# Preparing weight sums ahead of time: nine sets instead of seven, issued by GpSimd

## The chip, the cores and the metric

One core of a Trainium2 chip runs the whole program. The core has a matrix engine (PE in the profile), a vector engine (DVE), a scalar engine (ACT), GpSimd (POOL), and SyncE (SP), whose work here is to issue transfers. Every engine executes its own list of instructions strictly in order; what one engine must wait for from another, it waits for at a semaphore. Transfers run on 16 DMA engines, whoever issues them. The metric is the device time of one execution in microseconds (us), as the median of several executions; lower is better.

## The reference: what is computed

One transformer layer over 256 tokens of width 2048, in float32, with three kinds of attention that share one projection, gates, and a gated feed-forward part:

```
z   = split_cols(h @ w_in)                                   # queries, keys, values, gates
mix = g_fox * (fox(z) @ w_br_fox) + g_nsa * (nsa(z) @ w_br_nsa) + g_dsa * (dsa(z) @ w_br_dsa)
h   = layer_norm(ALPHA * h + mix @ w_out)
a, b = split(h @ w_ffn_in, 2)                                # each 5632 columns
h   = layer_norm(ALPHA * h + (silu(a) * b) @ w_ffn_out)
h   = h + (p @ w_ple_in) * sigmoid(h @ w_ple_gate)
```

What this case is about is the product `h @ w_ffn_in` and what the attention stage does ahead of time for it.

## The kernel before, in words

**Precision and the triple product.** Every float32 operand is split into a high half and a low half (`halves`, L154: ACT copies the high half, DVE subtracts it to get the low half). A product is then three matmuls: high x high, low x high, high x low. All weights pass through this split, so DVE and ACT have work for each weight tile that PE uses.

**Groups of weights.** `gemm` (L207) walks through the 2048 rows of a weight matrix in groups of two blocks of 128 rows (1024 columns of a tile, or 768 where the matrix is 384 columns wide). For each group it loads the raw weights (`weight_group`, L158, on SP's queue), splits them and issues the matmuls. At the end of each group it calls `tick()` (L182), which lets side work advance by one step. Side work is written as Python generators: `yield n` means "come back n groups later". So one group of weights is the unit in which all side work is spread. The attention stage has 121 groups: 57 of the chunks c1 to c7, 48 of the chunks f0 to f5 (one for each fox head) and 16 of `gates(0)`. The lists `side` (attention heads and the like, three at a time) and `beside` (the preparation) hold the generators.

The program text gives the order of priority only. The order in which each engine's list is finally written is fixed at compile time by a planner that may move an instruction ahead of others on its engine when it expects its operands to be there. So side work can run well before the group at which it is written.

**Pairs with seven products.** `pair_gemm` (L279) multiplies the same input by two weight matrices at once (for the feed-forward part, 512 columns of `a` and 512 columns of `b`, a "chunk"). It takes the 2048 rows as eight pairs `p` of 128-row blocks. For each pair there are 2 x 2 blocks of tokens and rows, and 2 weight matrices: eight block products, 24 matmuls, in the plain way (`plain`, L340). For the pairs named in `seven` it uses a scheme with seven block products (L391 to L397), 21 matmuls. In exchange, sums and differences of weights have to be formed and split: four DVE additions (L380 to L382) and more `halves`.

The feed-forward part has chunks 0 to 10. Chunk 0 is made by `first_chunk`; chunks 1 to 10 by `next_chunk` (L1205), which chooses the pairs that go the seven-product way: `SEVEN` = (2, 4, 6) for chunk 1, `SEVEN_MOST` = (2, 3, 4, 5, 6) for a chunk that has a prepared set, and `SEVEN_MORE` = (2, 4, 5, 6) otherwise.

**Prepared sets.** For some chunks the sums of pair 2 are formed early, in the attention stage, by `prepare` (L891), and kept in DRAM. One set (c, p) takes three tiles of 128 x 1024 floats, `preb`, `prea` and `pret`: two loads of 512 KB (L898), four DVE sums (L900, L901, L903, L904), four splits of 128 x 512 (L907, L916, on ACT and DVE), three stores (L912 twice at 256 KB, L913 at 512 KB), and two more stores of 512 KB (L920). The feed-forward chunk then loads four ready tiles of 512 KB (L369) and one and a half raw ones (L329, L330: 256 KB and 512 KB).

The sets are in three lists (L41). The first list takes its tiles from the pool `k4`, and starts at group 26 (`PREPARE_FROM`, L924). The second uses the pool `gp` with three tiles, the third the pool `ka`; both start when the task `T["v"]` is done (L949), which, counted through the generators, is at group 57. Since each list has room for one set, or little more, the next set's loads must wait until the stores of the last one have landed. The number of groups that a set takes is the sum of its yields, 6 + 1 + 1 + 1 + 1 + 1 + 3 + 1 + 1 + 1 + 1 = 18. At the end, L966 runs whatever side work is left.

**Who issues.** In the kernel before, all loads and stores of `prepare` stand in SP's queue, between the loads of the weight groups (L168). GpSimd does next to nothing in the attention stage. Its few instructions there include small copies (L511) of one element from the newest low half of the weights into a tile that is about to be loaded. Such a copy computes nothing: it makes the load that follows wait until the weights have come that far (`newest`, set in L231).

Of the kernel before, what the change touches and what calls it, by code (L numbers as in the profile page):

```python
# [10 lines left out]
F32 = mybir.dt.float32  # L11
# [26 lines left out]
STAY, AHEAD = 1, 1  # L38

SEVEN_MOST = (2, 3, 4, 5, 6)  # L40
PREPARED, PREPARE_FROM = (((4, 2), (5, 2)), ((6, 2), (7, 2), (8, 2)), ((9, 2), (10, 2))), 26  # L41
NCMP = 15
PSUM = bass.MemoryType.PSUM

# [84 lines left out]
def build(ctx: ExitStack, tc: tile.TileContext, A: dict):  # L129
    nc = tc.nc  # L130
    PE, DVE, ACT, POOL = nc.tensor, nc.vector, nc.scalar, nc.gpsimd
# [22 lines left out]
    def halves(src, hi, lo):  # L154

        split_last[:] = [ACT.activation(hi, src, AF.Copy).ins, DVE.tensor_sub(lo, src, hi.bitcast(F32)).ins]  # L156
# [18 lines left out]
    side, beside, now, newest = [], [], [0], [None]  # L175
# [285 lines left out]
    with ExitStack() as at:  # L461
# [429 lines left out]
        def prepare(jobs, pool, tag, after=None):  # L891

            while after and not T[after]["done"]:
                yield 1
            for c, p in jobs:
                rb, ra, t = (pool.tile([P, 2, 512], F32, name=f"pre{x}", tag=tag) for x in "bat")
                for r, n in ((rb, 11 + c), (ra, c)):
                    nc.sync.dma_start(r, A["ffn_in"][n][:, 2 * p:2 * p + 2, :])  # L898
                yield 6
                DVE.tensor_sub(t[:, 0, :], rb[:, 0, :], rb[:, 1, :])  # L900
                DVE.tensor_sub(t[:, 1, :], rb[:, 0, :], ra[:, 0, :])  # L901
                yield 1
                DVE.tensor_sub(rb[:, 1, :], rb[:, 1, :], t[:, 1, :])  # L903
                DVE.tensor_sub(ra[:, 1, :], ra[:, 1, :], rb[:, 1, :])  # L904
                yield 1
                for i, r in enumerate((rb, ra)):
                    halves(t[:, i, :], r[:, 0, :].bitcast(F32R), t[:, i, :].bitcast(F32R))  # L907
                    yield 1
                yield 1
                d = prepared.setdefault(c, {})[p] = dram.tile([P, 8, 512], F32, name="pre")  # L910
                for i, r in enumerate((rb, ra)):
                    nc.sync.dma_start(d[:, i:i + 1, :], r[:, 0:1, :])  # L912
                nc.sync.dma_start(d[:, 2:4, :], t)  # L913
                yield 3
                for r in (rb, ra):
                    halves(r[:, 1, :], r[:, 0, :].bitcast(F32R), r[:, 1, :].bitcast(F32R))  # L916
                    yield 1
                yield 1
                for i, r in enumerate((rb, ra)):
                    nc.sync.dma_start(d[:, 4 + 2 * i:6 + 2 * i, :], r)  # L920
                yield 1

        T = {}
        beside.append({"gen": prepare(PREPARED[0], k4, "k4"), "at": PREPARE_FROM})  # L924
        lf_task = add(later_load())
        ps = chunk("c1", x=X_first, sizes=[[1], [1]])
# [21 lines left out]
        for i, (pool, tag) in enumerate(((gp, "g"), (ka, "ka"))):  # L948
            beside.append({"gen": prepare(PREPARED[1 + i], pool, tag, "v"), "at": 0})  # L949
# [432 lines left out]
```

## Time and profile before

| | |
|---|---|
| median of 3 runs | 1564.12 us (1563.99 to 1565.78) |
| the profiled execution: its own time | 1562.82 us |
| its span, first to last instruction | 1560.9 us |
| PE busy | 1545.5 us (99%) |
| DVE busy | 1367.2 us (88%) |
| ACT busy | 881.8 us (56%) |
| POOL busy | 20.1 us (1%) |
| DMA | 360.91 MB, mean 231 GB/s |
| granted TensorE clock | 1.000 |

The profile's page gives each engine's busy time, then the costliest groups of instructions by line; `out<-in` names the tiles. The trace behind it can be asked for windows (busy time of each engine in a stretch of time), for the waits of one engine (who waited for whom, total, number of times, longest), and for the timeline (start, duration, engine, line, operation, tiles; in brackets the idle time of the engine just before and what ended it). "SPq" and "POOLq" are issues in an engine's queue. Busy time of PE counts overlapping, pipelined matmuls, so it says that PE had work and not how fast it went; for the rate one looks at the distance from one matmul's start to the next.

The stages on the time axis: attention up to about 377 us (the first matmul of `pair_gemm` starts at 376.7 us), the gates and the mixing up to about 690 us, then the output projection, the feed-forward input (chunks 0 to 10), the feed-forward output and the last gate.

### The profile page before, as it was taken

To read this page: it belongs to the slowest core of one execution; us is meant where nothing else is said; L and a number is where in the kernel's file an instruction comes from. 1 tells how busy PE (TensorE), PEld (TensorE's weight loads), DVE (VectorE), ACT (ScalarE), POOL (GpSimd) and SP (SyncE) were. 2 spreads that over 40 slices of the span, in tenths; PEclk is the share of its full clock that TensorE was granted. 3 is DMA by queue.
4 is the path that set the end of the run, shared out by engine and by line. 5 is a ranking of instruction groups with operands and counts; after the bars stand their busy time and mean duration, and the time that the engine had idled before them with its cause. 6 is when DMAs were issued, how large, how long until landed. Compare 5 with 4: busy or idle time off the path is not lost. (4 is left out here: it accounts for less than half of the span.)

```text
span 1560.9 us, 20529 instructions
## 1 busy us (share of the span) xinstructions
PE 1545.5 (99%) x7314; PEld 1286.8 (82%) x7314; DVE 1367.2 (88%) x1914; ACT 881.8 (56%) x1155; POOL 20.1 (1%) x44
## 2 busy tenths in 40 slices
PE   9999999999999999999999999999999999999998
PEld 7778899998888888888788888888888888887887
DVE  6779787559898998998879999999999999989896
ACT  5545566556565555544455566656565666555463
POOL 1000000000000000001000000000000000010000
PEclk9999999999999999999999999999999999999999
DMA  8866988566645664658566667777777776886554
GB/s 284 303 215 211 302 284 283 169 209 206 237 158 192 216 236 158 229 172 265 160 219 214 229 213 245 262 263 271 266 261 275 245 267 229 290 289 251 166 171 135
DMA packets 105574, 360.91 MB, mean 231 GB/s; under 512 B 12032, under 2 KB 13184, under 8 KB 105472
## 3 DMA queue, kind: packets, MB, share of 16 engines
q1 hardware_dynamic: 104192, 355.41, 67.2%
q0 software_dynamic: 1280, 4.20, 0.9%
q8 instruction: 57, 0.93, 0.2%
q14 instruction: 45, 0.37, 0.1%
HBM read 337.54 MB, written 22.02 MB: 230 GB/s over the span
## 5 line engine op out<-in xcount | busy, mean ns | idle before, releaser
L156 DVE TENSOR_TENSOR wlo<-raw,whi 128x1024 fp32r<-128x1024 f32 (+3 forms) x539 | 586.7, 1104 | 131.8 <-ACT whi L156 128.0
L156 ACT ACTIVATE whi<-raw 128x1024 fp32r<-128x1024 f32 (+3 forms) x539 | 507.5, 962 | 338.3 <-PE acc L245 99.5
L244 PE MATMUL acc<-whi,k4h 128*128 128x512 f32 (+3 forms) x724 | 274.2, 379 | 1.8 <-ACT k4h L156 1.5
L246 PE MATMUL acc<-wlo,k4h 128*128 128x512 f32 (+3 forms) x724 | 267.0, 370 | 1.1 <-DVE wlo L156 1.1
L245 PE MATMUL acc<-whi,k4l 128*128 128x512 f32 (+3 forms) x724 | 267.2, 369 | 0.6 <-DVE k4l L156 0.6
L156 ACT ACTIVATE wthi<-raw 128x1024 fp32r<-128x1024 f32 x168 | 177.8, 1060 | 149.7 <-DVE raw L380 80.8
L156 DVE TENSOR_TENSOR wtlo<-raw,wthi 128x1024 fp32r<-128x1024 f32 x168 | 202.7, 1219 | 0.0
L297 PE MATMUL sc<-whi,k4h 128*128 128x512 f32 x489 | 191.6, 392 | 0.0
L298 PE MATMUL sc<-whi,k4l 128*128 128x512 f32 x489 | 190.5, 390 | 0.0
L299 PE MATMUL sc<-wlo,k4h 128*128 128x512 f32 x489 | 190.2, 390 | 0.1
L297 PE MATMUL acc<-whi,k4h 128*128 128x512 f32 x401 | 157.4, 393 | 0.3 <-ACT whi L156 0.3
L299 PE MATMUL acc<-wlo,k4h 128*128 128x512 f32 x401 | 156.4, 390 | 0.9 <-DVE wlo L156 0.9
L244 PEld LDWEIGHTS acc<-whi,k4h 128*128 128x128 f32 x724 | 136.1, 188 | 25.7 <-issue 4.7
L298 PE MATMUL acc<-whi,k4l 128*128 128x512 f32 x401 | 156.1, 389 | 0.0
L246 PEld LDWEIGHTS acc<-wlo,k4h 128*128 128x128 f32 x724 | 135.9, 188 | 21.5 <-DVE wlo L156 3.0
L245 PEld LDWEIGHTS acc<-whi,k4l 128*128 128x128 f32 x724 | 136.3, 188 | 18.7 <-DVE k4l L156 1.3
L380 DVE TENSOR_TENSOR raw<-raw 128x1024 f32<-128x1024 f32 x79 | 96.3, 1220 | 14.5 <-DMA raw<-ffn_out 5.9
L299 PEld LDWEIGHTS sc<-wlo,k4h 128*128 128x128 f32 x489 | 91.8, 188 | 19.9 <-DVE wlo L156 0.5
L297 PEld LDWEIGHTS sc<-whi,k4h 128*128 128x128 f32 x489 | 91.9, 188 | 18.8
L298 PEld LDWEIGHTS sc<-whi,k4l 128*128 128x128 f32 x489 | 91.8, 188 | 18.8
L299 PEld LDWEIGHTS acc<-wlo,k4h 128*128 128x128 f32 x401 | 75.2, 188 | 17.6 <-DVE wlo L156 1.9
L297 PEld LDWEIGHTS acc<-whi,k4h 128*128 128x128 f32 x401 | 75.3, 188 | 15.8 <-ACT whi L156 0.7
(370 smaller groups left out, 2120.4 us busy)
## 6 DMA issues: line engine op xcount, KB each, us to landing
raw<-ffn_in SPq DMA_DIRECT2D x169, 512.0 KB, 4.6
raw<-gate SPq DMA_DIRECT2D x96, 512.0 KB, 4.5
raw<-ffn_out SPq DMA_DIRECT2D x88, 512.0 KB, 5.0
raw<-att_c SPq DMA_DIRECT2D x40, 512.0 KB, 4.7
raw<-att_f SPq DMA_DIRECT2D x48, 384.0 KB, 3.8
raw<-ple_gate SPq DMA_DIRECT2D x32, 512.0 KB, 4.2
g<-actd SPq DMA_DIRECT2D x20, 512.0 KB, 5.0
g<-cmp SPq DMA_DIRECT2D x16, 512.0 KB, 5.6
```

What stands on the lines that cost most here:

```text
L156: split_last[:] = [ACT.activation(hi, src, AF.Copy).ins, DVE.tensor_sub(lo, src, hi.bitcast(F32)).ins]
L244: PE.matmul(o, xh[:, c], h, start=(k == 0), stop=False)
L245: PE.matmul(o, xl[:, c], h, start=False, stop=False)
L246: PE.matmul(o, xh[:, c], l, start=False, stop=(k == kt - 1))
L297: PE.matmul(o, xh, h, start=first, stop=False)
L298: PE.matmul(o, xl, h, start=False, stop=False)
L299: PE.matmul(o, xh, l, start=False, stop=stop)
L380: DVE.tensor_tensor(t[0], raw[:, 0:1, :].broadcast_to([P, 2, 512]), raw[:, 1:3, :], op=ALU.subtract)
```

## The change

Three things are changed.

1. The three lists hold three sets each: (2, 2), (3, 2), (4, 2) in `k4`; (5, 2), (6, 2), (7, 2) in `gp`; (8, 2), (9, 2), (10, 2) in `ka`. So chunks 2 and 3 get a prepared set too, and with it `SEVEN_MOST` in place of `SEVEN_MORE`: their pair 3 goes the seven-product way. The first list starts at group 20 instead of 26.
2. All seven transfers of a set are issued by GpSimd instead of SP, and each of the two loads has in front of it a one-element GpSimd copy from the newest low half of the weights into the tile.
3. The wait between a set's loads and its first sum is 4 groups instead of 6, so that a set takes 16 groups instead of 18.

```diff
-PREPARED, PREPARE_FROM = (((4, 2), (5, 2)), ((6, 2), (7, 2), (8, 2)), ((9, 2), (10, 2))), 26
+PREPARED, PREPARE_FROM = (((2, 2), (3, 2), (4, 2)), ((5, 2), (6, 2), (7, 2)), ((8, 2), (9, 2), (10, 2))), 20
@@ prepare
                 for r, n in ((rb, 11 + c), (ra, c)):
-                    nc.sync.dma_start(r, A["ffn_in"][n][:, 2 * p:2 * p + 2, :])
-                yield 6
+                    POOL.tensor_copy(r[:1, 0, :1], newest[0].bitcast(F32)[:1, :1])
+                    nc.gpsimd.dma_start(r, A["ffn_in"][n][:, 2 * p:2 * p + 2, :])
+                yield 4
...
                 for i, r in enumerate((rb, ra)):
-                    nc.sync.dma_start(d[:, i:i + 1, :], r[:, 0:1, :])
-                nc.sync.dma_start(d[:, 2:4, :], t)
+                    nc.gpsimd.dma_start(d[:, i:i + 1, :], r[:, 0:1, :])
+                nc.gpsimd.dma_start(d[:, 2:4, :], t)
...
                 for i, r in enumerate((rb, ra)):
-                    nc.sync.dma_start(d[:, 4 + 2 * i:6 + 2 * i, :], r)
+                    nc.gpsimd.dma_start(d[:, 4 + 2 * i:6 + 2 * i, :], r)
```

## The prediction, made before the result was known

> **What bounds the kernel now.** I read the page first, for the busy shares, then windows of the two stages that the change touches, and there the waits of PE.
>
> ```profile
> span 1560.9 us, 20529 instructions
> PE 1545.5 (99%) x7314; PEld 1286.8 (82%) x7314; DVE 1367.2 (88%) x1914; ACT 881.8 (56%) x1155; POOL 20.1 (1%) x44
> ```
>
> PE has work for nearly the whole span. Whether it also goes at its full rate is read from the distance between starts:
>
> ```profile
> 1100.21 0.39 PE L297 MATMUL sc<-whi,k4h 128*128 128x512 f32 x1
> ...
> 1102.93 0.39 PE L297 MATMUL sc<-whi,k4h 128*128 128x512 f32 x1
> ```
>
> These two starts lie 12 matmuls apart, so one 512-column matmul takes 2.72 / 12 = 0.227 us of PE's time; the 0.39 us of each is its length, and they overlap. The windows of the feed-forward stage (columns: length, then busy time of PE, PEld, DVE, ACT, POOL, clock, DMA share, GB/s):
>
> ```profile
> 880.00:900.00 20.00, 20.00 (x90) 16.57 (x89) 19.68 (x24) 11.87 (x15) 0.00 (x0) 1.00 0.63 211
> 1100.00:1120.00 20.00, 20.00 (x94) 16.57 (x93) 19.14 (x24) 11.58 (x15) 0.00 (x0) 1.00 0.84 295
> 1120.00:1140.00 20.00, 20.00 (x90) 16.57 (x89) 20.00 (x22) 13.32 (x15) 0.00 (x0) 1.00 0.67 230
> ```
>
> PE is never idle there; 88 x 0.227 = 20 us, so some 90 starts in 20 us are its rate. DVE is close behind: 19.1 to 20.0 of 20 us. The first row is from chunk 2 or 3 (no prepared set), the others from later chunks with one. The bound is PE, with DVE second. In the attention stage:
>
> ```profile
> 0.00:60.00 60.00, 56.88 (x261) 47.29 (x262) 42.72 (x83) 33.85 (x54) 5.88 (x19) 1.00 0.88 297
> 180.00:240.00 60.00, 58.22 (x346) 54.46 (x347) 50.91 (x145) 37.54 (x90) 0.00 (x0) 1.00 0.87 286
> 300.00:345.00 45.00, 45.00 (x252) 42.30 (x251) 24.16 (x41) 24.16 (x47) 0.00 (x0) 1.00 0.63 183
> PE sc L578 <- DVE p L574: 1.7, 2, 1.1
> PE sc L559 <- ACT fq L554: 1.0, 1, 1.0
> PE sc L553 <- ACT rf L859: 0.8, 1, 0.8
> PE sc L805 <- issue: 0.6, 1, 0.6
> ```
>
> The last four lines are all waits of PE between 100 and 345 us: 4.1 us, none of them for a weight load. So what can be had is little: fewer matmuls, or part of these 4.1 us.
>
> **Part 1: two more chunks with five seven-product pairs.** Chunks 2 and 3 get what chunks 4 to 10 have. Each loses 24 - 21 = 3 matmuls, 3 x 0.227 = 0.68 us. The trace has this price a second time. `leave` (L312) runs once in each chunk, after pair 6:
>
> ```profile
> 888.96 0.59 ACT L312 COPY g<-sc 128x512 f32<-128x512 f32 x1 [1.35 <-PE sc L299]
> 930.70 0.59 ACT L312 COPY g<-acc 128x512 f32<-128x512 f32 x1 [1.35 <-PE acc L299]
> 971.77 0.59 ACT L312 COPY g<-sc 128x512 f32<-128x512 f32 x1 [0.79 <-PE sc L299]
> 1012.84 0.59 ACT L312 COPY g<-acc 128x512 f32<-128x512 f32 x1
> ```
>
> Chunk 3, without a prepared set, lies between the first two: 41.74 us. Chunks 4 and 5 follow: 41.07 us each. The difference is 0.67 us, all costs included: DVE forms as many sums as before (four pairs on the fly either way), and the extra reading (four ready tiles and 0.75 MB raw in place of 1 MB: 1.75 MB in 41 us, 43 GB/s) fits, since the later chunks run at 230 to 295 GB/s without idle PE. Two chunks: **-1.34 us**. Bounds: -1.36 by matmuls; 0 if DVE, at 19.7 of 20 us in chunks 2 and 3, takes over.
>
> **Part 2: two more sets in the attention stage.** The work of a set:
>
> ```profile
> L900 DVE TENSOR_TENSOR pret<-preb x7: 672/689/697, 36.6 to 258.9; 128x512 f32<-128x512 f32 x7
> L156 DVE TENSOR_TENSOR preb<-preb x7: 684/689/693, 60.9 to 266.1; 128x512 fp32r<-128x512 f32 x7
> L156 ACT ACTIVATE preb<-preb x7: 625/632/635, 60.3 to 265.4; 128x512 fp32r<-128x512 f32 x7
> ```
>
> Four sums and four low halves on DVE, 8 x 0.69 = 5.5 us; four high halves on ACT, 4 x 0.63 = 2.5 us; 3 MB moved. Two more sets: 11 us of DVE, 5 us of ACT and 6 MB. Cover: DVE is busy 24.16 of 45 us at the end of the stage and 50.91 of 60 in its fullest window, the DMA engines 63 to 88%. So I cost this at nothing; without cover it would be 11 us.
>
> What matters is where it falls. Of `pret` alone DVE has five instructions a set:
>
> ```profile
> 120.00:180.00 60.00, 3.28 (x5) 1.16 (x2) 1.00 0.74 242
> 180.00:240.00 60.00, 13.01 (x20) 4.80 (x8) 1.00 0.87 286
> 240.00:300.00 60.00, 3.35 (x5) 1.16 (x2) 1.00 0.73 235
> raw<-att_f SPq DMA_DIRECT2D x48, 384.0 KB, 3.8
> L168 SPq DMA_DIRECT2D raw<-att_f x48: 327/328/415, 180.0 to 315.7; - x48
> ```
>
> Four of the seven sets are crowded into 180 to 240 us, just where DVE is fullest; the last split of `preb` starts at 266.1. 48 groups of the fox chunks load from 180.0 to 315.7 us, 135.7 / 47 = 2.9 us a group. With the new copy a set's loads can't run ahead of their group, and with the lists in threes the sets lie at groups 20, 36, 52 and, in twos, at 57, 73, 89, ending at 105. Group 57 is where the fox chunks begin, so the last six sets spread over all 48 of their groups, and some three fall into 180 to 240 us instead of four. The tiles of `gp` are wanted again at group 113, 8 x 2.9 = 23 us later: no new wait there.
>
> **Part 3: the 1.7 us.** What PE waited for at L578 shows on DVE:
>
> ```profile
> 222.46 0.16 DVE L572 TENSOR_TENSOR rr<-rr,g_nsa 128x2 f32<-128x2 f32 x1
> 224.74 0.69 DVE L900 TENSOR_TENSOR pret<-preb 128x512 f32<-128x512 f32 x1 [2.12 <-DMA preb<-ffn_in]
> 225.35 0.54 DVE L574 TENSOR_SCALAR p<-p,rr 128x128 f32<-128x128 f32 x2
> 227.88 0.33 PE L578 MATMUL sc<-ident,p 128*128 128x128 f32 x1 [1.10 <-DVE p L574]
> 211.96 0.63 SPq L920 DMA_DIRECT2D pre<-preb  x1
> 218.10 0.42 SPq L898 DMA_DIRECT2D preb<-ffn_in  x1
> ```
>
> A first sum of `prepare` sat 2.12 us on DVE, waiting for its load; the softmax step L574 of the NSA heads was queued behind it, and PE behind that. The load was late because its tile came free only when the last set's store had landed: issued at 211.96, load at 218.10 (6.1 us), data at 224.74 (6.6 us), 12.8 us in all. The new spacing leaves, from the last store (group 15 of 16) to the next first sum, 1 + 4 = 5 groups, 5 x 2.9 = 14.5 us: enough by 1.7 us if GpSimd is as quick as SP. And at group 57, whose sums fall near the NSA heads, no earlier set stands before the loads in those pools. Against it: the planner may still put a sum too early. I keep three quarters of this wait, in the proportion of sets in that window (three for four): **-0.4 us**; bounds -1.7 (gone) and, with more such collisions, +1.7 each.
>
> **Part 4: the issue moves from SP to GpSimd.**
>
> ```profile
> L1086 POOL DMA_DIRECT2D gb<-ln_b x8: 536/537/544, 709.2 to 1386.0; - x8
> 711.28 0.54 POOL L1086 DMA_DIRECT2D gb<-ln_b  x1
> 711.32 1.22 DVE L156 TENSOR_TENSOR wlo<-raw,whi 128x1024 fp32r<-128x1024 f32 x1
> DMA to landing us min/median/max: 4.4/7.2/9.3
> DMA to landing us min/median/max: 4.8/6.2/7.9
> ```
>
> 63 transfers at 0.54 us are 34 us of an engine with 1% of work. The last two lines are landing times of GpSimd's 256 KB loads (L1086) and of SP's 512 KB loads of `prepare` (L898): 7.2 and 6.2 us, so GpSimd costs about 1 us more, and the 1.7 us of slack shrink to 0.7. SP loses 49 issues, but no wait of PE above names a load, so that gives 0; the bound from below is the 0.6 us put down to issue. The new copy waits for a low half on DVE; behind it on GpSimd stand the loads, later stores and the memset L694, for which DVE's L695 waits. DVE may not rewrite that low half until the copy has read it: four buffers, 4 x 2.9 = 11.6 us, against some 7 us for which a store's landing can hold GpSimd. I take 0; a miss costs up to the 1.7 us of the one collision seen.
>
> [...]
>
> **The sum.** -1.34 - 0.4 = -1.7 us. The profiled execution took 1562.82 us, 1.9 more than its span; it becomes 1561.1. The median of the runs, 1564.12, lies 1.3 us above it; on that I predict 1562.4.
>
> **Rivals.** *The collisions go.* Sets no longer run ahead of their groups, DVE is freer, and at least half of PE's 4.1 us of waits disappears: -1.34 - 2.05 = -3.4, 1560.7; with all of them 1558.7. For it: the spacing above, and that only one wait of the four has `prepare` as its cause speaks against more. *DVE waits for more loads, slower.* Each start of a set is a place where an early sum can hold DVE. There are six such moments (groups 20, 36, 52, 57, 73, 89). With n of them costing PE 1.7 us as the one now does, the change is -1.34 + 1.7 (n - 1); it turns against us at n = 2 and passes 0.2% at n = 4: +3.8, 1567.9. For it: the slack of 0.7 us, and groups of 2.9 us that may get shorter as waits go; against: only one of seven sets cost PE anything before. *GpSimd's issues are starved by DVE.* If each issue waited for one DVE instruction, 1.22 us, two loads come 2.4 us late, the chain exceeds its 14.5 us, and all six starts collide: -1.34 + 8.5 = +7.2, 1571.3. [...] *The chunks do not gain*, as DVE is their bound after all: only the 0.4 remains, 1563.7.
>
> **How the numbers follow.** Forecast 0.45; collisions gone 0.29; more DVE waits 0.10; starved issues 0.04; no gain in the chunks 0.12. About 0.2% (3.1 us) is what a measurement can tell from no change. Faster by more: most of the second case and a tail of the first, 0.26. Slower by more: the third and fourth case with little left off, 0.13. Within: 0.61. The range leaves out all four waits gone below and n = 4 above: 1559.8 to 1566.6.
>
> **What would show it.** After: the L312 starts of chunks 1 to 5 all 41.07 us apart; 6 matmuls fewer; `prepare` instructions on DVE until about 330 us; GpSimd issues of 0.54 us; PE's waits between 100 and 345 us at 3 to 4 us. I am wrong if chunk 3 stays at 41.7 us, if PE waits on DVE's softmax steps add up to 6 us or more, or if issues on GpSimd take over 1 us.

## The result, and the profile after

The changed kernel takes 1574.89 us (median of 6 runs, 1571.46 to 1576.79), against 1564.13 us of the kernel before. The ratio is 1.0063, with a 95% interval of 1.005 to 1.0077: slower by 8 to 12 us, where 1.7 us faster was predicted. The profiled execution took 1574.61 us, with a span of 1572.8 us.

The page of the kernel after begins with the busy times of its engines:

```profile
span 1572.8 us, 20695 instructions
PE 1548.0 (98%) x7308; PEld 1287.8 (82%) x7308; DVE 1372.4 (87%) x1930; ACT 884.2 (56%) x1163; POOL 56.4 (4%) x125
```

Six matmuls fewer, as the change intends, and POOL's busy time is up by 36.3 us: its issues and copies. The first question is in which stage the time went. The first matmul of `pair_gemm` marks the end of the attention stage, and the `leave` copies (L312) mark the chunks:

```profile
387.50 0.39 PE L297 MATMUL sc<-whi,k4h 128*128 128x512 f32 x1
...
859.94 0.57 ACT L312 COPY g<-acc 128x512 f32<-128x512 f32 x1
900.90 0.59 ACT L312 COPY g<-sc 128x512 f32<-128x512 f32 x1 [1.30 <-PE sc L299]
941.97 0.59 ACT L312 COPY g<-acc 128x512 f32<-128x512 f32 x1
```

Before, that first matmul started at 376.7 us. So 10.8 us are lost in the attention stage, before any chunk begins. Chunks 2 and 3 now take 40.96 and 41.07 us, against 41.64 and 41.74 before; the gain that was promised there is real. Another 1.8 us are lost between the first two of these lines, and 0.6 us behind the last; where, is not followed here. In the attention stage, PE's waits between 100 and 345 us are these (total, number, longest), 10.9 us in all, against 4.1 before:

```profile
PE sc L553 <- DVE ra L546: 3.2, 1, 3.2
PE sc L553 <- ACT rf L859: 2.6, 2, 1.5
PE sc L805 <- DVE gu L801: 2.2, 2, 2.0
PE sc L559 <- ACT fq L554: 1.8, 1, 1.8
PE sc L559 <- DVE rr L570: 0.9, 1, 0.9
PE sc L578 <- DVE p L574: 0.2, 1, 0.2
```

The names are those of attention steps, not of `prepare`: one has to ask what stood ahead of these steps. DVE's waits for the loads of a set grew from 3.8 us (2 times) to 15.6 us; in the kernel after the first two sums are lines L901 and L902:

```profile
DVE pret L901 <- DMA preb<-ffn_in: 12.1, 6, 3.8
DVE pret L902 <- DMA prea<-ffn_in: 3.5, 5, 1.1
```

The costliest place, in the timeline of all engines:

```profile
191.15 0.53 POOL L899 DMA_DIRECT2D preb<-ffn_in  x1
191.68 0.54 POOL L899 DMA_DIRECT2D prea<-ffn_in  x1
192.20 0.53 POOL L899 DMA_DIRECT2D preb<-ffn_in  x1
192.72 0.53 POOL L899 DMA_DIRECT2D prea<-ffn_in  x1
...
197.98 0.69 DVE L901 TENSOR_TENSOR pret<-preb 128x512 f32<-128x512 f32 x1 [3.84 <-DMA preb<-ffn_in]
...
202.08 0.69 DVE L901 TENSOR_TENSOR pret<-preb 128x512 f32<-128x512 f32 x1 [0.63 <-DMA preb<-ffn_in]
...
202.69 0.28 DVE L542 TENSOR_TENSOR ra<-acc,cst 128x128 f32<-128x128 f32 x1
...
203.65 0.30 PE L553 MATMUL sc<-ident,ra 128*128 128x128 f32 x1 [3.15 <-DVE ra L546]
```

Two lists start a set at the same group, so GpSimd starts four loads of 512 KB within 1.6 us. DVE has the first sum next on its list, and waits 3.84 us for its load; the splits and the rotation steps L542 to L546 are queued behind it, and PE waits 3.15 us for the last of those. The windows around that moment (length, then busy time of PE, PEld, DVE, ACT, POOL, clock, DMA share, GB/s) show a second price:

```profile
200.00:204.00 4.00, 0.85 (x6) 0.56 (x6) 3.01 (x13) 2.85 (x6) 1.10 (x2) 1.00 0.94 369
204.00:208.00 4.00, 4.00 (x16) 3.91 (x15) 3.77 (x7) 2.35 (x6) 0.96 (x2) 0.57 0.53 164
```

PE works for only 0.85 of the first 4 us. In the next 4 its granted clock is 0.57 on average, that is 0.5 for 3.4 us and 1 for the rest; in these 3.4 us the 384-column matmuls start 0.32 us apart, behind them 0.17. The L246 matmuls there, from 204.14 to 207.91 us, fall another 1.6 us behind those of the kernel before, and one wait of 3.2 us, with what followed it, costs 4.9 (the lag between 199 and 209 us, below).

The second costly place is near 320 us. There it is ACT that waits, for ordinary weights (`whi <- raw`); L859 is queued behind, and PE waits for that (ACT's timeline, then PE's):

```profile
318.07 0.85 ACT L156 ACTIVATE whi<-raw 128x768 fp32r<-128x768 f32 x1 [2.04 <-DMA raw<-att_f]
318.82 0.35 ACT L859 COPY rf<-acc 128x256 f32<-128x256 f32 x1
...
321.54 0.84 ACT L156 ACTIVATE whi<-raw 128x768 fp32r<-128x768 f32 x1 [2.20 <-DMA raw<-att_f]
...
326.06 0.84 ACT L156 ACTIVATE whi<-raw 128x768 fp32r<-128x768 f32 x1 [3.25 <-DMA raw<-att_f]
```

```profile
322.70 0.44 PE L553 MATMUL sc<-ident,rf 128*128 128x128 f32 x2 [1.12 <-ACT rf L859]
327.22 0.49 PE L559 MATMUL sc<-fq 128*128 128x128 f32 x2 [1.75 <-ACT fq L554]
```

The transfers in flight just before, between 310 and 322 us (queue, packets, MB, share of the 16 engines' time; then issues with their median landing):

```profile
q0 software_dynamic: 729, 2.68, 57.1%
q1 hardware_dynamic: 544, 1.47, 37.7%
...
raw<-att_f SPq DMA_DIRECT2D x5, 384.0 KB, 5.8
```

q0 carries what GpSimd issues, q1 what SP issues: from before to after q0 grows from 4.20 to 32.51 MB, that is by the 28.3 MB of nine sets. While GpSimd's stores are under way, the weights get 38% of the DMA engines and land after 5.8 us, against 4.4 us as the median of all 48. That median is no worse than with SP as issuer (4.5 us in e1, below), so the weights are late in places only.

The stores act in another way too. The second split of a set, on ACT, writes over the half of `preb` that is being stored, so it must wait until that store has landed. GpSimd issued it at 122.52 us; ACT waits, its attention step L799 stands behind, and PE waits for what DVE makes of L799's output:

```profile
128.10 0.63 ACT L156 ACTIVATE preb<-preb 128x512 fp32r<-128x512 f32 x1 [3.61 <-DMA pre<-preb]
...
133.25 0.60 PE L805 MATMUL sc<-cmp,gu 128*15 128x128 f32 x4 [1.98 <-DVE gu L801]
```

With the L246 matmuls of the two kernels set side by side in their order, the lag behind the kernel before grows by 1.4 us near 85 us, by 4.9 between 199 and 209, and by 3.4 between 321 and 329. Elsewhere it goes up and down, by some 4 us where the two kernels write their steps in another order, and 1.3 us of that stay.

### The profile page after: what moved, and what is told of

Same layout as the page of the kernel before. It is cut to its first block, busy times and chain, and to the rows that moved or that the text cites. A ratio compares the mean times of both kernels' runs of the same rounds, so it can differ in the third digit from the quotient of the medians.

```text
span 1572.8 us, 20695 instructions
## 1 busy us (share of the span) xinstructions
PE 1548.0 (98%) x7308; PEld 1287.8 (82%) x7308; DVE 1372.4 (87%) x1930; ACT 884.2 (56%) x1163; POOL 56.4 (4%) x125
## 3 DMA queue, kind: packets, MB, share of 16 engines
q0 software_dynamic: 9200, 32.51, 5.7%
## 4 chain that ended last, share of the span: by engine, by line
PE 76%; DMA 9%; DVE 7%; issue 5%; ACT 2%; POOL 0%; SPq 0%; ACTq 0%; DVEq 0%; POOLq 0%
PE sc L297 9%; PE sc L299 9%; PE sc L298 9%; PE acc L299 8%; PE acc L298 8%; PE acc L297 8%; PE acc L244 6%; PE acc L246 6%; PE acc L245 6%; DVE wlo L156 3%; DMA raw<-att_c 3%; DMA preb<-ffn_in 2%; ACT whi L156 2%; DMA raw<-w_out 1%; DVE wtlo L156 1%
## 5 line engine op out<-in xcount | busy, mean ns | idle before, releaser
L246 PE MATMUL acc<-wlo,k4h 128*128 128x512 f32 (+3 forms) x724 | 267.6, 371 | 1.8 <-DVE wlo L156 1.8
L297 PE MATMUL sc<-whi,k4h 128*128 128x512 f32 x483 | 189.3, 392 | 0.0
L297 PE MATMUL acc<-whi,k4h 128*128 128x512 f32 x395 | 155.1, 393 | 1.3 <-ACT whi L156 1.3
L246 PEld LDWEIGHTS acc<-wlo,k4h 128*128 128x128 f32 x724 | 136.5, 189 | 22.5 <-DVE wlo L156 3.8
L297 PEld LDWEIGHTS sc<-whi,k4h 128*128 128x128 f32 x483 | 90.7, 188 | 18.6
L299 PEld LDWEIGHTS acc<-wlo,k4h 128*128 128x128 f32 x395 | 74.1, 188 | 16.9 <-DVE wlo L156 1.5
L297 PEld LDWEIGHTS acc<-whi,k4h 128*128 128x128 f32 x395 | 74.2, 188 | 16.7 <-ACT whi L156 1.8
```

The costliest lines, as they stand in the source:

```text
L246: PE.matmul(o, xh[:, c], l, start=False, stop=(k == kt - 1))
L297: PE.matmul(o, xh, h, start=first, stop=False)
L299: PE.matmul(o, xh, l, start=False, stop=stop)
```

## The experiments

Ratios are to the kernel before, run beside each kernel on the same chip, with 95% intervals; a difference in us is (ratio - 1) x 1564. "End" is the start of the first L297 matmul in the profile, "half" the time before it in which PE's clock was granted at 0.5. Both are of one profiled execution, which need not be a typical one: e5's is the fastest of its 10 (1565.6 us, the median is 1571.9), those of e15 and e16 lie 4.5 and 3.5 us above their medians.

| kernel | ratio (interval) | end | half |
|---|---|---|---|
| before | 1 | 376.7 | 0 |
| the change | 1.0063 (1.005 to 1.0077) | 387.5 | 3.4 |
| e1: all on SP | 1.0004 (0.9992 to 1.0016) | 376.1 | 0 |
| e2: no copies | 1.0114 (1.0095 to 1.0132) | 394.2 | 3.4 |
| e3: seven sets | 1.0037 (1.0026 to 1.0048) | 380.3 | 0 |
| e4: sums held 4 groups | 1.0045 (1.0032 to 1.0059) | 384.2 | 3.4 |
| e5: loads alone on GpSimd | 1.005 (1.0035 to 1.0066) | 381.1 | 3.4 |
| e6: stores alone on GpSimd | 1.0014 (1.0001 to 1.0028) | 379.8 | 0 |
| e7: before, issued by GpSimd | 1.0124 (1.0097 to 1.015) | 389.5 | 6.8 |
| e8: third list 6 groups later | 1.0122 (1.0107 to 1.0137) | 398.5 | 17.0 |
| e9: as e4, all on SP | 1.0029 (1.0016 to 1.0043) | 379.3 | 0 |
| e10: as e4, loads alone on GpSimd | 1.0037 (1.0022 to 1.0052) | 380.5 | 6.8 |
| e11: as e1, no copies | 1.003 (1.0016 to 1.0043) | 380.7 | 3.4 |
| e12: as e1, loads issued by ACT | 1.0046 (1.003 to 1.0062) | 385.4 | 3.4 |
| e13: sums held 3 groups, all on SP | 0.9998 (0.9984 to 1.0012) | 376.8 | 0 |
| e14: as e13, all on GpSimd | 1.0062 (1.0039 to 1.0084) | 385.9 | 6.8 |
| e15: as e1, seven sets | 1.0009 (0.9995 to 1.0024) | 379.3 | 3.4 |
| e16: as e1, 18 groups a set | 1.001 (0.9997 to 1.0023) | 380.4 | 3.4 |
| e17: as e13, loads alone on GpSimd | 1.0046 (1.0031 to 1.0061) | 381.5 | 3.4 |
| e18: as e13, stores alone on GpSimd | 1.0046 (1.0029 to 1.0063) | 386.3 | 3.4 |

**Which part of the change costs: e1, e2, e3, e4.** Three theories stood at first: A, the first sums stand on DVE ahead of their loads' landing, since the copies hold the loads back; B, transfers cost more when GpSimd issues them; C, two more sets are simply more work.

e1 takes the issue back to SP and keeps the rest:

```diff
-                    nc.gpsimd.dma_start(r, A["ffn_in"][n][:, 2 * p:2 * p + 2, :])
+                    nc.sync.dma_start(r, A["ffn_in"][n][:, 2 * p:2 * p + 2, :])
...
-                    nc.gpsimd.dma_start(d[:, i:i + 1, :], r[:, 0:1, :])
-                nc.gpsimd.dma_start(d[:, 2:4, :], t)
+                    nc.sync.dma_start(d[:, i:i + 1, :], r[:, 0:1, :])
+                nc.sync.dma_start(d[:, 2:4, :], t)
...
-                    nc.gpsimd.dma_start(d[:, 4 + 2 * i:6 + 2 * i, :], r)
+                    nc.sync.dma_start(d[:, 4 + 2 * i:6 + 2 * i, :], r)
```

> The changed kernel with the seven transfers of a set issued by SP again; the one-element copies, nine sets and 16 groups stay. Theory A (a set's first sums stand in DVE's order before their loads have landed, since the copy holds the loads back to their group and the planner puts the sums too early): the copies are still there, so DVE still waits 10 us or more for these loads and the time stays at 1570 to 1576 us. Theory B (GpSimd is a slow issuer): DVE's waits for loads fall to about the 4 us of before, 1562 to 1566 us. Theory C (the two extra sets are simply more work than DVE and ACT can hide): 1572 to 1576 us, with DVE's waits for loads small.

Measured: no difference from the kernel before (1564.9 us), and DVE waits only 2.4 us for loads of a set. Nine sets, copies and the shorter spacing are all still there, so theory C falls, and the loss hangs on the issuer. The two landing rows between 50 and 330 us, first of the change, then of e1:

```profile
preb<-ffn_in POOLq DMA_DIRECT2D x9, 512.0 KB, 7.3
prea<-ffn_in POOLq DMA_DIRECT2D x9, 512.0 KB, 8.3
```

```profile
preb<-ffn_in SPq DMA_DIRECT2D x9, 512.0 KB, 5.3
prea<-ffn_in SPq DMA_DIRECT2D x9, 512.0 KB, 6.1
```

The same load, issued under the same copies, lands 2.0 to 2.2 us later from GpSimd. The other pairs that differ in the issuer show less. Over all kernels with copies the two medians are 6.0 to 7.3 and 6.6 to 8.3 us from GpSimd, and 5.0 to 6.2 and 6.1 to 6.9 us from SP. In e3 (GpSimd) they are 6.0 and 6.6, in e15, the same seven sets on SP, 5.6 and 6.6; yet e3 is 4.4 us slower than e15. So a later landing is not the whole cause.

e2 leaves out the copies:

```diff
-                    POOL.tensor_copy(r[:1, 0, :1], newest[0].bitcast(F32)[:1, :1])
```

> The changed kernel without the one-element copies ahead of the loads; GpSimd issues, nine sets, 16 groups. Theory A: the loads run ahead of their groups again, DVE waits at most 5 us for them, 1562 to 1567 us. Theory B: GpSimd is as slow as before, 1572 to 1576 us. Theory C: 1572 to 1576 us.

It is 18 us slower than before, more than any of the theories had, though DVE waits only 1.3 us for loads of a set. So the copies are not the fault; on GpSimd they are needed. What they hold back is seen in e7.

e3 goes back to seven sets from group 26:

```diff
-PREPARED, PREPARE_FROM = (((2, 2), (3, 2), (4, 2)), ((5, 2), (6, 2), (7, 2)), ((8, 2), (9, 2), (10, 2))), 20
+PREPARED, PREPARE_FROM = (((4, 2), (5, 2)), ((6, 2), (7, 2), (8, 2)), ((9, 2), (10, 2))), 26
```

> The changed kernel with the old lists: seven sets, from group 26; GpSimd issues, copies, 16 groups. So the feed-forward chunks have the 1.3 us less gain. Theory A: seven starts in place of nine, DVE waits some 10 to 12 us for loads, 1570 to 1575 us. Theory B: the same, 1570 to 1575 us. Theory C: back to 1563 to 1566 us.

5.8 us slower than before, 4 less than the change: with GpSimd as issuer the two further sets cost something.

e4 holds the two first sums behind the newest weight split, so that DVE can't take them up earlier than the group at which they are written:

```diff
-                DVE.tensor_sub(t[:, 0, :], rb[:, 0, :], rb[:, 1, :])
-                DVE.tensor_sub(t[:, 1, :], rb[:, 0, :], ra[:, 0, :])
+                with tc.issue_after(split_last[1]):
+                    DVE.tensor_sub(t[:, 0, :], rb[:, 0, :], rb[:, 1, :])
+                    DVE.tensor_sub(t[:, 1, :], rb[:, 0, :], ra[:, 0, :])
```

> The changed kernel, with the two first sums of a set held on DVE behind the newest weight split at the point where they are written, four groups after the loads; nothing else changes. Theory A: DVE waits less than 4 us for the loads, PE's waits between 60 and 345 us go back to 3 to 5 us, and the time is 1561 to 1565 us. Theory B: loads of GpSimd are later than four groups, the waits and the time stay, 1572 to 1576 us. Theory C: 1570 to 1576 us with small waits for loads.

DVE's waits for loads of a set are gone, and 7 of 10 us of the loss are still there (1572.7 us). That seems to refute theory A, but does not: the hold costs 4.5 us by itself (e9, below), and of the 7 us only 2.5, good to some 3 us, are left for GpSimd's transfers.

**Loads or stores: e5, e6.** From here theory L is A with B's reason: the load lands 2 us later, and the sums stand on DVE as if it didn't. Q, W and G are told in the expectations. The edits are those lines of e1's diff that concern the stores (e5) or the loads (e6).

> The change with only the two loads of a set (and their one-element copies) on GpSimd; the five stores go back to SP. Theory L (a load that GpSimd issues lands about 2 us later than one that SP issues, 7.3 and 8.3 us against 5.3 and 6.1 us, and the set's first sums stand on DVE ahead of that moment, so DVE and behind it PE wait): all of the loss stays, 1571 to 1575 us, DVE waits of 10 us or more for the sets' loads before 390 us. Theory Q (GpSimd runs its list in order, and stores that wait for splits hold back the copies and loads behind them): with loads alone in its list nothing holds them back, 1564 to 1567 us. Theory W (the order that the planner writes for DVE and ACT is worse when it plans transfers on GpSimd): in between, with DVE waits for loads but also changed waits on other steps.

> The change with only the five stores of a set on GpSimd; the two loads go back to SP, their one-element copies stay. Theory L: the loads land after 5 to 6 us again, DVE waits for them 3 us at most, and the time is that of the version with all transfers on SP, 1564 to 1566 us. Theory Q: the copies still stand behind stores in GpSimd's list, so the loads still come late in part, 1568 to 1572 us. Theory W: 1568 us or more without DVE waits for loads.

Loads alone cost 7.8 us and stores alone 2.2. In e5 DVE waits 7.8 us for loads of a set, and 6.7 us more at the same sums that the profile puts down to nothing ("issue"). That speaks for L and against Q, whose mark was a healed e5. e6 lies between the marks of L and Q, with 1567.4 us and 4.4 us of such waits. PE's matmuls stand in the same order in e6 as in the change, as far as the traces have them (some records are missing), and e6 still gives most of the time back; so the order on PE is not the cause.

**The issuer alone, and fewer at once: e7, e8.** e7 is the kernel before with the four `dma_start` lines of `prepare` on `nc.gpsimd`. e8 is the change with a later third list:

```diff
-            beside.append({"gen": prepare(PREPARED[1 + i], pool, tag, "v"), "at": 0})
+            beside.append({"gen": prepare(PREPARED[1 + i], pool, tag, "v", 6 * i), "at": 0})
```

where the new last argument is a number of groups to wait after `T["v"]`.

> The kernel before with nothing changed but the issuer: seven sets, starting at group 26, 18 groups each, no one-element copies, all transfers of a set issued by GpSimd. Theory L: without the copies the loads are issued as early as their tiles come free and the first sums stand 6 groups behind instead of 4, so most of the loss is gone: 1564 to 1567 us. Theory that the issue by GpSimd costs by itself, however early the loads go (its queue, or its transfers beside the weight loads): 1569 us or more.

> The change with the third list started 6 groups after the second, so that no two sets load at the same moment; all else as in the change. Theory G (two sets' four loads are issued within 2 us, 2 MB at once, so the fourth lands after 10 us and the weight loads among them land late; DVE and ACT wait for that): the longest DVE wait for a load falls from 3.8 us to under 2 us and 4 to 8 us come back, 1566 to 1570 us. Theory L: each load still lands after some 7 us and is waited for, now at nine moments instead of six: 1572 to 1577 us.

Both miss what L and G expected, and by far: 19 us slower each. e7 falls to its other theory, that the issue by GpSimd costs by itself (1569 us or more); no theory had e8. For e7 the timeline suggests why: the first load of a set, in e7 and then in the kernel before:

```profile
1.31 0.69 POOL L898 DMA_DIRECT2D preb<-ffn_in  x1 [0.43 <-issue]
```

```profile
28.04 0.42 SPq L898 DMA_DIRECT2D preb<-ffn_in  x1
```

In SP's queue the load takes its turn among the weight loads, at 28 us. GpSimd has nothing else on its list, and sends it off at 1.3 us, beside the constants and the first weights. The second set's loads go out at 53.1 and 53.7 us, and ACT waits for a weight beside them, in e7:

```profile
58.78 1.06 ACT L156 ACTIVATE whi<-raw 128x1024 fp32r<-128x1024 f32 x1 [4.26 <-DMA raw<-att_c]
61.97 0.45 PE L553 MATMUL sc<-ident,rc 128*128 128x128 f32 x1 [3.46 <-DVE rc L546]
```

The one-element copies hold GpSimd back: in the change its first load goes out at 55.0 us, right behind a split of its group. e8 has the loads of the two lists apart, and DVE still waits 16.9 us for them, now at more moments; a good part of its loss is the clock. Its windows with a clock under 1 (the clock is the third number from the end):

```profile
130.00:145.00 15.00, 12.69 (x53) 9.80 (x52) 11.25 (x33) 6.67 (x8) 1.78 (x4) 0.89 0.74 247
220.00:236.00 16.00, 11.36 (x57) 10.25 (x56) 12.37 (x46) 10.63 (x33) 1.64 (x3) 0.79 0.61 202
318.00:340.00 22.00, 18.14 (x86) 17.24 (x86) 11.64 (x17) 9.71 (x19) 2.71 (x5) 0.84 0.79 278
```

17 us at half clock before the end of the stage, so some 8 us lost of the 21.8 by which the stage ends later (an estimate from the 0.32 and 0.17 us above), on top of the waits themselves.

**GpSimd, or only another queue: e12.** e1's kernel with the two loads issued by ACT:

```diff
-                    nc.sync.dma_start(r, A["ffn_in"][n][:, 2 * p:2 * p + 2, :])
+                    nc.scalar.dma_start(r, A["ffn_in"][n][:, 2 * p:2 * p + 2, :])
```

> Nine sets, copies on GpSimd, stores on SP, the two loads of a set issued by ACT. If what matters is that a load from GpSimd itself lands late, loads from ACT land after 5 to 6 us like SP's and the time is 1563 to 1567 us, unless ACT loses time waiting for the copies. If what matters is that the loads leave SP's queue, where they take turns with the weight loads, it is as slow as with the loads on GpSimd: 1570 us or more, and landing times of 6.5 us or more.

As slow as with the loads on GpSimd (7.2 against 7.8 us). Its landing rows and DVE's waits:

```profile
preb<-ffn_in ACTq DMA_DIRECT2D x9, 512.0 KB, 6.3
prea<-ffn_in ACTq DMA_DIRECT2D x9, 512.0 KB, 6.9
```

```profile
DVE pret L901 <- DMA preb<-ffn_in: 14.4, 4, 5.7
DVE pret L902 <- DMA prea<-ffn_in: 2.9, 4, 1.1
```

So the loss does not need GpSimd. Whether it needs a late landing is less clear: 6.3 and 6.9 us are 0.8 to 1.0 us more than in e1, but no more than in e18, whose loads SP issues (6.2 and 6.9). ACT also issues late, between its other work: near 239 us all four copies are done at 239.6, and the four loads go out at 239.2, 241.4, 243.6 and 243.9. So e12 does not tell a second queue from ACT's own delay. My reading, argued and not shown, is that in SP's queue a load goes ahead of the weight loads issued after it, and that on a second queue it shares the DMA engines with them. The shares of 57.1% and 37.7% above show both queues served in the same 12 us, which fits, but not in what turns.

**The sums held, issuer by issuer: e9, e10, then e13, e14, e17, e18.** e9 and e10 are e4 with all transfers, or the stores alone, on SP. In the other four the hold is 3 groups long:

```diff
-                yield 4
+                yield 3
...
                     nc.gpsimd.dma_start(d[:, 4 + 2 * i:6 + 2 * i, :], r)
-                yield 1
+                yield 2
```

> All transfers on SP, one-element copies, nine sets, and the two first sums of a set held behind the newest weight split. The control for the version with GpSimd's transfers and held sums (1572.7 us). If holding the sums costs by itself (sums pushed into later, fuller places on DVE), this one is slow too, 1568 us or more. If holding is free, 1562 to 1566 us, and then the 8 us of the held GpSimd version are put down to GpSimd's transfers by another way than a sum that waits for its load.

> As the version before it, but the two loads on GpSimd (stores on SP). Theory L (the loss comes from the first sums that wait on DVE for a load that lands 2 us later): no such wait is left, so the time is that of the version on SP with held sums, within 2 us. Theory that the loads from GpSimd disturb others (they land later because they share the DMA engines with the weight loads otherwise): 5 us or more slower than that version, as it is without the hold (1571.9 against 1564.9 us).

> Nine sets, copies, all transfers on SP, the first sums held behind the newest split 3 groups after the loads instead of 4. Control for the next one. If the 3 us of the longer hold come from sums pushed into fuller places, the shorter hold costs less: 1564 to 1567 us.

> The same with all transfers on GpSimd: the sums stand some 8.7 us after the loads' issue, where the loads of a single set (6.2 to 8.3 us) have landed and the last ones of two sets (up to 10.6 us) have not. Theory L (the loss is the sums that wait on DVE): 1566 to 1570 us, DVE waits for loads under 4 us before 390 us in place of 15.6 us. Theory that GpSimd's transfers cost 7 us whatever the sums do: 1571 us or more, as with the 4-group hold (1572.7 us).

> Nine sets, copies, first sums held 3 groups back, the loads on GpSimd and the stores on SP. If loads from GpSimd cost only by the sums that wait for them, this one is within 2 us of all on SP (1565.2 us): 1564 to 1567 us. If they cost by making weight loads late, 1570 us or more.

> The same with the loads on SP and the stores on GpSimd. If the stores are the second path (they go out beside the weight loads and make those late, so ACT and behind it PE wait), most of the 10 us are here: 1570 to 1575 us, and ACT waits for weights near 310 to 320 us. If not, 1564 to 1567 us, and then loads and stores cost only together.

With 4 groups the hold by itself costs 4.5 us (e9), and the loads on GpSimd add only 1.3 to that (e10; each interval is 2 us to either side), as L expected. With 3 groups it is free (e13). But e14 then has nearly the whole loss, 9.7 us, with DVE waits of 3.7 us for loads, where L expected 6 us at most. So L is not the whole either. e17 and e18 put 7.2 us on the loads alone and 7.2 on the stores alone: not a sum of parts, but with this hold each way of taking transfers out of SP's order is enough. Each kernel set against the one that differs from it only in that SP issues everything (us, good to 3 or 4):

| issued by GpSimd | sums free (e1) | seven sets (e15) | held 4 groups (e9) | held 3 groups (e13) |
|---|---|---|---|---|
| all transfers | 9.2 | 4.4 | 2.5 | 10.0 |
| the loads | 7.2 | not run | 1.3 | 7.5 |
| the stores | 1.6 | not run | not run | 7.5 |

The stores can also make the weights late. Transfers during two sets' stores, in e14 (306 to 322 us) and in e13 (298 to 316 us):

```profile
q0 software_dynamic: 764, 2.80, 44.1%
q1 hardware_dynamic: 817, 2.23, 41.8%
...
raw<-att_f SPq DMA_DIRECT2D x6, 384.0 KB, 5.7
```

```profile
q1 hardware_dynamic: 1815, 5.11, 86.9%
...
raw<-att_f SPq DMA_DIRECT2D x8, 384.0 KB, 4.9
```

The weights land after 5.7 us beside GpSimd's stores, after 4.9 among SP's. Over the whole stage this shows in e18, where ACT waits 50.8 us for attention weights against 37.2 in e13, but not in the change, with 36.2 against 35.2 in e1.

**What the other parts give, all on SP: e11, e15, e16.** e11 is e1 without the copies; e15 is e1 with e3's lists; e16 is e1 with `yield 6`.

> Nine sets in 16 groups each, all transfers on SP, without the one-element copies: the lists alone. On GpSimd the copies were worth 10 us (1583.7 without, 1571 to 1575 with), since nothing else there keeps a load from running ahead. On SP the loads stand among the weight loads in the queue. If that order paces them, leaving out the copies changes little: 1563 to 1566 us. If the loads run far ahead of their group on SP too, 1568 us or more, and the attention stage shows weight loads that land late near 40 to 60 us.

> The kernel before with the one-element copies and 16 groups a set, seven sets from group 26, all transfers on SP. Against nine sets on SP (1564.9 us) it lacks 1.36 us in chunks 2 and 3 and saves two sets of work in the attention stage. If the extra sets are hidden, as the prediction had it, this one is 1.4 us slower than the nine, 1566 us; if they cost what the chunks give, the same, 1565 us; if they cost more, faster, 1563 us or less.

> Nine sets with copies on SP, with the old 6 groups between loads and sums, so 18 groups a set, the last ending at group 111. If the remaining DVE waits for loads (2.4 us with 16 groups) go with the longer spacing and nothing else gets late, the time is that of the 16-group version or up to 1.5 us better, 1563 to 1565 us, and would be the best version. If the planner puts the sums early all the same, nothing changes; slower than 1566 us would mean that the third list now collides with the end of the stage.

e11 came out at the slower of its two branches: the copies are worth 4 us on SP too. Seven sets (e15), nine (e1) and nine with 18 groups each (e16) can't be told apart, at 1.4, 0.6 and 1.6 us with intervals of about 2 us to each side. The extra sets are hidden, or cost no more than chunks 2 and 3 give.

No version beats the kernel before by more than a measurement tells; e1 and e13 equal it.

## Why the prediction was wrong, point by point

**Part 1 was right.** Chunks 2 and 3 took 40.96 and 41.07 us; against 41.64 and 41.74 before, 1.35 us were gained, 1.34 predicted, by the mechanism that was named.

**Part 2 was right only on SP.** With SP as issuer, two more sets cost nothing that shows (e1, e15). With GpSimd they cost 4 us more than they give (1.0063 against 1.0037); that it is because each brings more transfers beside the weights is likely, and not shown.

**Part 3 failed in "I keep three quarters of this wait".** The working followed the chain from a set's last store to its next load, and that chain was relieved. But the new copy ties the load to the newest weights, so that what counts is now the time from the load's issue to DVE's arrival at the sum. The working took 4 groups of 2.9 us for it; at the three moments when two lists load together (sums at 198.0, 245.6 and 295.2 us) DVE came to the first sum 2.2 to 3.0 us after the issue. That "the planner may still put a sum too early" stood there as an aside; it is what happened. It did so with GpSimd as issuer: with the same copies and SP (e1) DVE's waits are 2.4 us in place of 15.6.

**Part 4 is the step that failed: "I take 0".** The issue itself was sized rightly:

```profile
L899 POOL DMA_DIRECT2D preb<-ffn_in x9: 527/532/713, 55.0 to 291.9; - x9
```

0.53 us each beside a busy DVE and 0.71 at most, so the issues were not starved. "About 1 us more" for the landing compared two kinds of load from different stages; for the same load it is 2 us in the change against e1, and 0 to 1.5 us in the other pairs. So its size was not far off. What failed is that nothing was taken to follow from it: "no wait of PE above names a load, so that gives 0" looked at waits in a kernel where all transfers stood in one order. PE does not wait for a load here either; it waits for DVE and ACT, and these wait for a set's loads (3.84 us at 198 us), for its stores (3.61 us at 128 us) and for weights (3.25 us at 326 us). Moving all seven transfers out of SP's queue cost 9.2 us where 0 was taken (change against e1).

**The price of a wait was too low.** 1.7 us per collision had no room for the clock. At 200 us a wait of 3.2 us cost 4.9.

**The rivals.** *DVE waits for more loads, slower* named the right engine, the right wait and the six moments, and got 0.10; its 1567.9 us for four collisions was too low, as it had one path of the two and no clock. The range ended at 1566.6, 8 us short. *Issues starved* came nearest in time (1571.3), but no run shows its term, an issue that waits 1.22 us for DVE: the issues of `prepare` in the change took 0.53 to 0.56 us, and one 0.71. The sign that I set for being wrong, PE waiting on DVE's softmax, did not come (0.2 us at L574): PE waited mostly for a rotation (L546), for ACT's copies (L859, L554) and for L801.

**What stays open.** The planner writes a different order for each kernel, so two kernels differ by more than the issuer, and effects of the parts do not add: stores alone on GpSimd cost 2.2 us with free sums and 7.2 with sums held 3 groups, and all transfers on GpSimd cost next to nothing more than on SP when the sums are held 4 groups. Why, is open. That sharing the DMA engines with a second queue is the reason for these paths rests on the landing rows, whose ranges touch, on the shares and on e12, where ACT's own delay is a rival; a run in which only the sharing changes, at one fixed order of instructions, was not made.

## What to carry to other kernels

SP's queue, which carried the seven transfers of a set and the weight loads in one order, was also a schedule: taking the seven out of it cost 9.2 us (change against e1). So before moving bulk transfers to an idle engine's queue, ask which urgent loads they used to stand in one order with, and price a later landing for both (here 2 us for a set's loads, in the change against e1, and 5.7 us in place of 4.9 for the weights, in e14 against e13). The engine with nothing to do sent its transfers as early as it could (e7's first load at 1.3 us, at 28 us on SP), so what held them back must be replaced (here by one-element copies, worth 8 us on GpSimd and 4 on SP). Where PE is the bound, a gap can cost half as much again through the clock (4.9 us for 3.2 here), though it need not (behind gaps of 1.12 and 1.75 us, at 322.7 and 327.2 us of the change, the clock stayed at 1.00).

## What the hardware showed that was not expected

Some gaps behind which the clock was halved were short. Single waits of PE of 1.87 us (e10, near 218 us) and 2.08 us (e14, near 299 us) were followed by 3.4 us at half clock. In e13's output stage PE waited 1.56 and then 0.72 us, and the clock then fell; in e6, at the same place, 1.92 and 0.72 us, and it did not. The windows after these gaps, e13 and then e6:

```profile
1440.00:1443.00 3.00, 0.78 (x3) 0.30 (x2) 2.36 (x3) 3.00 (x4) 0.00 (x0) 1.00 0.04 16
1443.00:1447.00 4.00, 3.94 (x10) 3.15 (x11) 4.00 (x5) 2.34 (x3) 0.00 (x0) 0.57 0.17 24
```

```profile
1445.00:1448.00 3.00, 0.73 (x2) 0.30 (x2) 2.41 (x3) 3.00 (x4) 0.00 (x0) 1.00 0.04 16
1448.00:1452.00 4.00, 3.99 (x17) 3.30 (x18) 4.00 (x4) 2.30 (x3) 0.00 (x0) 1.00 0.18 37
```

All 20 profiles have this pair of waits, the first of 0.30 to 2.18 us and the second of 0.71 or 0.72, and in 8 of them the clock fell behind it for 3.4 us. e1 and e16 have the same pair, 1.01 and 0.72 us, and it fell in e1 alone. So the same pair of waits cost some 1.6 us in one run and nothing in another (an estimate from e13, where 512-column matmuls start 0.43 us apart at half clock and 0.23 us before it). Every stretch at half clock before the end of the attention stage lasted 3.4 or 6.8 us. What decides whether the clock falls, no run here shows; half clock followed 1.87 us alone in e10, and 1.01 us with 0.72 us in e1.
